# Three buffers, a later due time and copies in three pieces for the transposed convolution results of a two-layer hybrid block

## The chip, the cores and the metric

The kernel runs on one core of one Trainium2 chip. The time is the device time of one execution in microseconds (us). Three runs of the kernel before the change took 2925.31, 2929.0 and 2931.43 us; the median is 2929.0 us. One further execution was recorded by the hardware profiler, and all rows below come from it.

## The reference

Two layers (`DEPTH = 2`) work on 1024 latent tokens and 256 context tokens, each a vector of 1024. A layer normalizes and modulates its input, multiplies it by one wide matrix, splits the product in ten parts and feeds three branches: a state space scan (SSD) with a short convolution in front, attention with 12 query and 4 key heads, and a conformer branch with a long convolution. The branches are joined and multiplied by an output matrix. Cut to the part that the change touches:

```python
h = modulate(x, norm_g[i], shift[:, None], scale[:, None])
h_c = modulate(ctx, norm_g[i], shift_c, scale_c)
z, xbc, dtr, q, k, v, ga, ua, ub, gc = split_cols(h @ w_in[i])
...
# SSD branch: 1280 channels, a convolution of 5 taps along the tokens
xbc = jax.nn.silu(dwconv(xbc, conv_w, conv_b))
xs = xbc[..., :SSD_WIDTH].reshape(b, L, SSD_HEADS, SSD_HEAD_DIM)
Bm = xbc[..., SSD_WIDTH:SSD_WIDTH + SSD_BC]
Cm = xbc[..., SSD_WIDTH + SSD_BC:]
...
# conformer branch: 512 channels, a convolution of 31 taps
u = ua * jax.nn.sigmoid(ub)
u = jax.nn.silu(layernorm(dwconv(u, conv_w, conv_b), ln_g, ln_b))
u = u @ pw_w + pw_b
return u * jax.nn.silu(gate)
```

## The kernel before

All 1280 tokens (`T`) are held as ten tiles (`NT`) of 128. The normalized input lies in SBUF with its 1024 features on the partitions, in a high part `hh` and a low part `hl`, since every float32 product is built from three products of rounded parts (`mm3`, L193): for each of 8 slices of 128 features, high by high, high by low and low by high. Each result tile of 512 columns is thus 24 matmuls into one of the four PSUM buffers of the tag `m`.

Weights come through `wblock`. It loads a block in two halves: SP issues the DMA into a raw buffer `wr` (of which the pool has one), ScalarE copies it to the rounded high part (`wth`), and VectorE or GpSimd subtracts that to get the low part (`wtl`); `wth` and `wtl` have two buffers each. The second half's DMA waits until the raw buffer has been read.

A layer (`phase_b`) runs through these stages. First the k projection of ten token tiles, with weights (`wk`) from a pool of their own that was filled while the norms ran. Then that pool is closed (`ws.close()`) and two pools are opened on the same side of SBUF: `gp`, with the small buffers of gates and copies, and behind it `wt`, with the weights of all further projections. The v projection, a part with q and dt, and two parts of q follow; in between stand matmuls of the adaptive modulation (`ada_w`).

Then comes the convolution stage, nine blocks, alternately a pair of `xbc` tiles (128 channels each) and a pair `ub`, `ua`. The product of `xbc` is copied by ScalarE to a padded row `xpad`; `conv_x` (L557) makes five passes over it on VectorE into `xcv`, a tanh on ScalarE into `th`, and a last step on VectorE that multiplies the two. The products `ub` go through ScalarE's tanh into a tile of the same name and buffer `th` (one buffer), VectorE multiplies it by `ua` into `up`, and `conv_cm` makes 31 passes over `up` on VectorE into `cac`. Results 0 to 7 of `conv_x` are also transposed: TensorE turns ten squares of 128 by 128, four into a PSUM tile `x` (one buffer), four into `t` (two buffers) and two into `x` again; ScalarE copies them to SBUF, and DMAs take them to DRAM (`xt_d`, `bt_d`), from where the scan reads them by token. Gates (`g_t`, `g_o`), the tail of the conformer branch, the scan, attention and the output product come behind.

The order on each engine is not the order of the code. Every operation carries a due time in us, set by `at(...)`, and a list scheduler with a timeline of its own orders each engine's instructions by these. `XLAG` is the distance of a result's transposes from the due time of its convolution. Pools hand out buffers, and the waits between engines follow from which memory an operation reads and writes, also where a tile lies on memory that a closed pool had before.

Of the kernel before, what the change touches and what calls it, by code (L numbers as in the profile page):

```python
# [10 lines left out]
AF = mybir.ActivationFunctionType  # L11
# [18 lines left out]
A2B = 1  # L30
GATP = True
GB = 2
XLAG = 34
PVB = (4, 6)
DM = 1024
NLAT = 1024
# [2 lines left out]
NT = T // 128  # L39
# [121 lines left out]
def build(tc, a, out, depth=DEPTH, dump=None):  # L161
    nc = tc.nc
    es = ExitStack()
    V, S, G, P, Y = nc.vector, nc.scalar, nc.gpsimd, nc.tensor, nc.sync

    def at(us):
        tc.cur_priority = int(us * 100)

    def pool(st, name, bufs=1, **k):
        return st.enter_context(tc.tile_pool(name=name, bufs=bufs, **k))  # L170
# [3 lines left out]
    def mk(p, shape, tag, dt=F32, bufs=None):  # L174
        uid[0] += 1
        k = {} if bufs is None else {"bufs": bufs}
        return p.tile(shape, dt, tag=tag, name=f"{tag}_{uid[0]}", **k)
# [8 lines left out]
    def dr(shape, name, dt=F32):  # L186
        t = dp.tile(shape, dt, tag=name, name=name)
        if dump is not None:
            dump[name] = t
        return t  # L190
# [4 lines left out]
    def tr(o, i, idt):  # L195
        P.transpose(o, i, idt)  # L196

    def act(o, i, f, **k):
        S.activation(o, i, f, **k)  # L199

    def ts(e, o, i, s1, op0, s2=None, op1=None):
        if op1 is None:
            e.tensor_scalar(o, i, s1, None, op0)
        else:
            e.tensor_scalar(o, i, s1, s2, op0, op1)  # L205

    def stt(o, i, s, i1, op0, op1):
        V.scalar_tensor_tensor(o, i, s, i1, op0, op1)  # L208
# [24 lines left out]
    for l in range(depth):  # L233
        t = mk(cp, [128, NCOL], f"colc{l}")
        Y.dma_start(out=t, in_=a["colc"][l])
        colc.append(t)
        t = mk(cp, [128, NROW], f"rowc{l}")
# [18 lines left out]
    xt_d = dr([NT, 128, 768], "xt_d")  # L256
    bt_d = dr([NT, 128, 256], "bt_d")
# [176 lines left out]
    def phase_b(l, nh, b0, pp):  # L434
# [71 lines left out]
        gp = pool(st_r, f"gp{l}", side="right")  # L506
# [32 lines left out]
        xp_p = pool(s2, f"xp{l}")  # L539
# [17 lines left out]
        def conv_x(j, t0):  # L557
            xp = xps[j]
            at(t0)
            o = mk(xp_p, [128, 1282], "xcv", bufs=2)  # L560
            w = sw[:, 5 * j:5 * j + 5]
            ts(V, o, xp[:, 0:1282], w[:, 0:1], ALU.mult, sw[:, 50 + j:51 + j], ALU.add)
            for k in range(1, 5):
                at(t0 + 2 * k)
                stt(o, xp[:, k:k + 1282], w[:, k:k + 1], o, ALU.mult, ALU.add)
            at(t0 + 10)
            th = mk(up_p, [128, 1282], "th")
            act(th, o, AF.Tanh)
            stt(o, th, 1.0, o, ALU.add, ALU.mult)
            if j >= 6:  # L570
                d = bT_d[j - 6] if j < 8 else cT_d[j - 8]
                Y.dma_start(out=d[:, 0:1024], in_=o[:, 0:1024])
                Y.dma_start(out=d[:, 1024:1280], in_=o[:, 1026:1282])
            if j < 8:
                at(t0 + XLAG)
                sg = mk(gp, [128, NT, 128], "xsg")
                for ta in (0, 4, 8):
                    n = min(4, NT - ta)
                    ps = mk(*((pt, [128, 4, 128], "t") if ta == 4 else (px, [128, 4, 128], "x")))
                    for t in range(ta, ta + n):  # L580
                        c0 = t * 128 + (2 if t >= 8 else 0)
                        tr(ps[:, t - ta, :], o[:, c0:c0 + 128], idf)
                    act(sg[:, ta:ta + n, :], ps[:, 0:n, :], AF.Copy)
                if j < 6:
                    d = xt_d[:, :, 128 * j:128 * j + 128]
                else:
                    d = bt_d[:, :, 128 * (j - 6):128 * (j - 6) + 128]
                Y.dma_start(out=d.rearrange("t p f -> p t f"), in_=sg)

        def gate(ps, t0, n, d):  # L590
            th = mk(gp, [128, 512], "g_t", bufs=2)
# [31 lines left out]
        def block(i):  # L623
            u = FM_UNITS[i]
            u0 = b2 + 26 * i
            at(u0 - 20)
            w = wblock(wt, wt, a["wfm"][l, i], "wt", 2)
            tt = u0
            for m, (n, j) in enumerate(u):
                full = n == "xbc" or not last  # L630
                for t0, tn in ((0, 512), (512, 512), (1024, 256)):
                    if t0 >= 1024 and not full:
                        continue
                    at(tt)
                    ps = mk(pm, [128, 512], "m")
                    mm3(ps[:, 0:tn], lambda x, k: w[x][:, k, 128 * m:128 * m + 128],
                        lambda x, k: h[x][:, k, t0:t0 + tn], KT)
                    fm_fin(ps, n, j, t0, tn)
                    tt += 5.2 * tn / 512
                if n == "ua":  # L640
                    conv_cm(j, tt, CM_PACE)
                if n == "xbc":
                    conv_x(j, tt)
# [563 lines left out]
```

## Time and profile before

| what | value |
|---|---|
| median of three runs | 2929.0 us |
| profiled execution | 2925.86 us, span of its instructions 2924.0 us |
| TensorE busy | 2775.7 us, 95% of the span |
| VectorE busy | 2167.2 us, 74% |
| ScalarE busy | 1068.0 us, 37% |
| GpSimd busy | 1167.3 us, 40% |
| mean granted clock of TensorE | 0.976 of full speed |

Shares of busy time are means over the whole program. The convolution stage of layer 0 lies at about 250 to 600 us of the span, that of layer 1 at about 1770 to 2080 us; the v projections lie at about 98 us and 1655 us. The names in the rows are those of the program's tiles: `t<-msk,xcv` is a transpose of a convolution result into the PSUM tile `t` (a transpose is a matmul with an identity matrix, which lies in the tile `msk`), `m<-hh,wth` is a matmul of a projection into a tile `m`, `xsg<-x` is the copy of a transposed piece to SBUF. A time in square brackets is how long the engine stood idle before the instruction, with the operation that ended the wait.

### The profile page before, as it was taken

The page shows a single profiled execution, that of the slowest core. Times are in us where ns is not written, and L with a number is a line of the kernel's source. Part 1 is how long each engine was busy: PE and PEld are TensorE (multiplying, and loading weights), DVE is VectorE, ACT ScalarE, POOL GpSimd, SP SyncE. Part 2 cuts the span into 40 slices and gives each one's busy share as a digit, 9 for nine tenths or more (in the row PEclk, how much of TensorE's full clock was granted, in tenths as well). Part 3 has the DMA queues.
Part 4 walks back from the last instruction along what each step waited for, and adds up shares of the span by engine and source line. Part 5 has one row for each costly group of instructions (what it writes and reads, how often), then busy time and mean ns, then how long its engine had stood idle before and what let it go on. Part 6 is the DMA issues. An engine that isn't in the chain of part 4 may idle for free. (4 is left out here: it accounts for less than half of the span.)

```text
span 2924.0 us, 41060 instructions
## 1 busy us (share of the span) xinstructions
PE 2775.7 (95%) x15708; PEld 2058.5 (70%) x15708; DVE 2167.2 (74%) x2987; ACT 1068.0 (37%) x1801; POOL 1167.3 (40%) x832
## 2 busy tenths in 40 slices
PE   5999998999999999899999999999998999999998
PEld 3888876888855555565787998877886565555676
DVE  4576899973288889887545577999834889898744
ACT  4212221222245555454335322222223455644532
POOL 2244122232166767662112353122322676775111
PEclk8999998999999999999999999999999999999999
DMA  6541111223342323223745322113335232321654
GB/s 237 191 160 66 56 55 62 92 92 112 101 144 84 102 68 104 67 76 99 213 153 161 122 77 68 56 55 98 111 118 168 74 98 77 95 64 43 185 154 144
DMA packets 284035, 314.44 MB, mean 108 GB/s; under 512 B 27606, under 2 KB 219190, under 8 KB 282814
## 3 DMA queue, kind: packets, MB, share of 16 engines
q1 hardware_dynamic: 283838, 311.82, 33.5%
q8 instruction: 123, 2.02, 0.3%
q14 instruction: 74, 0.61, 0.1%
HBM read 236.25 MB, written 75.50 MB: 107 GB/s over the span
## 5 line engine op out<-in xcount | busy, mean ns | idle before, releaser
L193 PE MATMUL m<-hh,wth 128*128 128x512 f32 (+1 forms) x1440 | 534.9, 371 | 0.1
L193 PE MATMUL m<-hl,wth 128*128 128x512 f32 (+1 forms) x1440 | 533.4, 370 | 0.0
L193 PE MATMUL m<-hh,wtl 128*128 128x512 f32 (+1 forms) x1440 | 532.7, 370 | 0.0
L199 ACT ACTIVATE a_p<-m 128x512 f32<-128x512 f32 x492 | 289.0, 595 | 374.0 <-PE m L193 370.6
L208 DVE SCALAR_TENSOR_TENSOR cac<-up,cmw,cac 128x1295 f32<-128x1295 f32 (+1 forms) x240 | 385.4, 1627 | 2.0
L935 DVE TENSOR_REDUCE a_sm<-m 128x1 f32<-128x512 f32 (+1 forms) x600 | 332.5, 582 | 46.9 <-PE m L193 45.0
L359 POOL TENSOR_TENSOR wtl<-wr,wth 128x1024 fp32r<-128x1024 f32 x68 | 200.3, 2945 | 406.6 <-ACT wth L199 406.6
L193 PE MATMUL t<-a_p,vs 128*64 128x256 f32 x1968 | 324.0, 405 | 0.7 <-DVE a_rc L1010 0.3
L193 PEld LDWEIGHTS m<-hh,wth 128*128 128x128 f32 x1440 | 274.0, 190 | 48.0 <-ACT th L199 0.5
L193 PEld LDWEIGHTS m<-hh,wtl 128*128 128x128 f32 x1440 | 273.5, 190 | 48.3
L193 PEld LDWEIGHTS m<-hl,wth 128*128 128x128 f32 x1440 | 273.8, 190 | 47.4
L193 PE MATMUL m<-q_a,k_a 128*128 128x512 f32 (+1 forms) x656 | 259.7, 406 | 6.1 <-DVE a_sm L935 4.6
L193 PE MATMUL m<-k_a,q_a 128*128 128x512 f32 (+1 forms) x600 | 247.0, 437 | 13.6 <-DVE a_sm L935 9.8
L193 PE MATMUL m<-woh,yh 128*128 128x512 f32 x576 | 225.8, 395 | 8.2 <-issue 3.3
L193 PE MATMUL m<-woh,yl 128*128 128x512 f32 x576 | 228.8, 398 | 4.4 <-DVE yl L1099 4.3
L193 PE MATMUL m<-wol,yh 128*128 128x512 f32 x576 | 226.5, 394 | 0.0
L193 PE MATMUL m<-q_b,k_b 65*128 65x512 f32 (+1 forms) x656 | 218.8, 344 | 0.0
L193 PEld LDWEIGHTS m<-q_a,k_a 128*128 128x128 f32 x656 | 125.9, 192 | 107.1 <-issue 52.0
L193 PEld LDWEIGHTS t<-a_p,vs 128*64 128x64 f32 x1968 | 104.3, 136 | 133.9 <-issue 95.3
L193 PEld LDWEIGHTS m<-k_a,q_a 128*128 128x128 f32 x600 | 113.5, 195 | 113.3 <-issue 45.2
L199 ACT ACTIVATE wth<-wr 128x1024 fp32r<-128x1024 f32 (+1 forms) x84 | 89.3, 1064 | 256.3 <-DMA wr<-in_wfm 134.5
L193 PE MATMUL m<-wth,hh 128*128 128x256 f32 (+1 forms) x608 | 173.7, 288 | 0.6 <-DVE c_qn L474 0.5
(239 smaller groups left out, 5604.4 us busy)
## 6 DMA issues: line engine op xcount, KB each, us to landing
wr<-in_wfm SPq DMA_DIRECT2D x68, 512.0 KB, 3.6
s_cb<-cum_d SPq DMA_DIRECT2D x72, 384.0 KB, 3.7
ada_w<-in_adaw SPq DMA_DIRECT2D x32, 512.0 KB, 4.2
wor<-in_wout SPq DMA_DIRECT2D x64, 256.0 KB, 3.1
s_x<-xt_d SPq DMA_DIRECT2D x38, 384.0 KB, 3.0
yf<-ys_d SPq DMA_DIRECT2D x36, 384.0 KB, 4.0
yf<-ya_d SPq DMA_DIRECT2D x36, 384.0 KB, 4.2
yf<-yc_d SPq DMA_DIRECT2D x36, 256.0 KB, 2.9
```

Source lines behind the costliest of these rows:

```text
L193: P.matmul(o, l, r, start=start, stop=stop)
L199: S.activation(o, i, f, **k)
L208: V.scalar_tensor_tensor(o, i, s, i1, op0, op1)
L359: (e or G).tensor_tensor(lo[:, s], raw, hi[:, s].bitcast(F32), ALU.subtract)
L935: V.tensor_reduce(sm[:, 2 * x + t, j:j + 1], ps[:, 0:kn], axis=AX.X, op=ALU.max)
```

## The change

The due time of the transposes goes from 34 to 62 us behind the convolution's. `xcv` gets a third buffer. The tile `xsg` for a whole transposed result (ten squares, 5120 bytes per partition) goes; each of the three PSUM tiles is copied into a buffer of the tag `g_o`, of which there are two and which the gates use too (2048 bytes per partition each), and every piece has a DMA of its own.

```diff
-XLAG = 34
+XLAG = 62
...
-            o = mk(xp_p, [128, 1282], "xcv", bufs=2)
+            o = mk(xp_p, [128, 1282], "xcv", bufs=3)
...
             if j < 8:
                 at(t0 + XLAG)
-                sg = mk(gp, [128, NT, 128], "xsg")
+                if j < 6:
+                    d = xt_d[:, :, 128 * j:128 * j + 128]
+                else:
+                    d = bt_d[:, :, 128 * (j - 6):128 * (j - 6) + 128]
                 for ta in (0, 4, 8):
                     n = min(4, NT - ta)
                     ps = mk(*((pt, [128, 4, 128], "t") if ta == 4 else (px, [128, 4, 128], "x")))
                     for t in range(ta, ta + n):
                         c0 = t * 128 + (2 if t >= 8 else 0)
                         tr(ps[:, t - ta, :], o[:, c0:c0 + 128], idf)
-                    act(sg[:, ta:ta + n, :], ps[:, 0:n, :], AF.Copy)
-                if j < 6:
-                    d = xt_d[:, :, 128 * j:128 * j + 128]
-                else:
-                    d = bt_d[:, :, 128 * (j - 6):128 * (j - 6) + 128]
-                Y.dma_start(out=d.rearrange("t p f -> p t f"), in_=sg)
+                    sg = mk(gp, [128, 512], "g_o", bufs=2)[:, 0:128 * n].rearrange("p (t f) -> p t f", t=n)
+                    act(sg, ps[:, 0:n, :], AF.Copy)
+                    Y.dma_start(out=d[ta:ta + n].rearrange("t p f -> p t f"), in_=sg)
```

How the engines' orders change is seen at three places. The first is SP, the engine that issues the DMAs, at the end of layer 0's k projection: `wr_151` and `wr_152` are the two halves of the v weights, `k_d` the stores of finished k tiles, and behind each row stands what it waits for. Before:

```order
L278 DMA ada_w_389_2554<-in_adaw 128x1024 [waits DMAHW7_49,DMAHW3_49,PE_49]
L357 DMA wr_151_945<-in_wtm 128x1024 [waits DVE_49,DMAHW0_49,Activation_49,Pool_49]
L484 DMA k_d_127<-c_t1_129_809 128x256 [waits DMAHW1_49,DVE_49]
L484 DMA k_d_127<-c_t1_135_849 128x256 [waits DVE_49]
L278 DMA ada_w_390_2558<-in_adaw 128x1024 [waits DMAHW6_49,PE_49]
L278 DMA ada_w_391_2562<-in_adaw 128x1024 [waits DMAHW7_49,DMAHW4_49,PE_49]
L357 DMA wr_152_949<-in_wtm 128x1024 [waits DMAHW5_49,DMAHW0_49,DVE_49]
L484 DMA k_d_127<-c_t1_141_889 128x256 [waits DVE_49]
```

And now:

```order
L484 DMA k_d_127<-c_t1_129_809 128x256 [waits DMAHW0_49,DVE_49]
L484 DMA k_d_127<-c_t1_135_849 128x256 [waits DMAHW1_49,DVE_49]
L278 DMA ada_w_390_2558<-in_adaw 128x1024 [waits DMAHW6_49,PE_49]
L278 DMA ada_w_391_2562<-in_adaw 128x1024 [waits DMAHW7_49,PE_49]
L357 DMA wr_151_945<-in_wtm 128x1024 [waits PE_49,DMAHW4_49,Activation_49,Pool_49]
L484 DMA k_d_127<-c_t1_141_889 128x256 [waits DMAHW5_49,DVE_49]
L278 DMA ada_w_395_2574<-in_adaw 128x4x256 [waits DMAHW2_49,PE_49]
L278 DMA ada_w_396_2580<-in_adaw 128x4x256 [waits DMAHW3_49,PE_49]
L484 DMA k_d_127<-c_t1_147_929 128x256 [waits DMAHW0_49,DVE_49]
L308 DMA gt_d0_148<-ada_g_392_2566 2x1024 [waits DMAHW1_49,DVE_49]
L304 DMA ada_b_426_2727<-in_adab 2x1024
L357 DMA wr_152_949<-in_wtm 128x1024 [waits DMAHW4_49,DVE_49]
```

The first half's load stood ahead of two k stores and two `ada_w` loads and waited for VectorE, ScalarE and GpSimd; it now stands behind them and waits for TensorE, ScalarE and GpSimd. Its TensorE wait is for the last matmul of the k projection. Four more rows stand between the two halves.

The second place is TensorE in layer 0, where in the trace of before the wait at 352.77 us lies. `xcv_477` (now `xcv_481`) is the convolution result of channel tile 2, `xcv_487` (now `xcv_493`) that of channel tile 3, and `m` is a product of the next projection. Before:

```order
L193 MATMUL m_501_3499<-hh_19_153,wtl_494_3411 128x512
L196 MATMUL x_480_3284<-msk_2_74,xcv_477_3274 128x128 x4
L196 MATMUL t_481_3290<-msk_2_74,xcv_477_3274 128x128 x4
L196 MATMUL t_491_3399<-msk_2_74,xcv_487_3383 128x128 x4
L196 MATMUL x_482_3296<-msk_2_74,xcv_477_3274 128x128 x2
L193 MATMUL m_503_3529<-hh_19_153,wth_493_3410 128x512
```

And now:

```order
L193 MATMUL m_509_3515<-hh_19_153,wtl_502_3427 128x512
L196 MATMUL x_483_3291<-msk_2_74,xcv_481_3282 128x128 x4
L196 MATMUL t_485_3299<-msk_2_74,xcv_481_3282 128x128 x4
L196 MATMUL t_497_3412<-msk_2_74,xcv_493_3395 128x128 x4
L193 MATMUL m_511_3545<-hh_19_153,wth_501_3426 128x512
```

The last two squares of tile 2 (`x` x2) have left this place; they come some 170 rows later. The first pieces of tile 2 and the `t` piece of tile 3 stand where they stood.

The third place is TensorE where the wait at 493.94 us lies, with the results of channel tiles 6 and 7 (`xcv_549` and `xcv_559`, now `xcv_561` and `xcv_573`) and two long convolution results (`cac`). Before:

```order
L193 MATMUL m_573_4363<-hh_19_153,wtl_566_4275 128x512
L196 MATMUL x_552_4146<-msk_2_74,xcv_549_4134 128x128 x4
L196 MATMUL t_553_4152<-msk_2_74,xcv_549_4134 128x128 x4
L196 MATMUL x_554_4158<-msk_2_74,xcv_549_4134 128x128 x2
L196 MATMUL x_562_4257<-msk_2_74,xcv_559_4245 128x128 x4
L196 MATMUL t_563_4263<-msk_2_74,xcv_559_4245 128x128 x4
L196 MATMUL t_710_5641<-msk_2_74,cac0_429_2748 128x128
L196 MATMUL t_710_5641<-msk_2_74,cac1_430_2749 128x128
L193 MATMUL m_575_4393<-hh_19_153,wth_565_4274 128x512
```

And now:

```order
L193 MATMUL m_589_4395<-hh_19_153,wtl_582_4307 128x512
L196 MATMUL x_563_4169<-msk_2_74,xcv_561_4158 128x128 x4
L196 MATMUL t_565_4177<-msk_2_74,xcv_561_4158 128x128 x4
L196 MATMUL x_567_4185<-msk_2_74,xcv_561_4158 128x128 x2
L196 MATMUL x_575_4284<-msk_2_74,xcv_573_4273 128x128 x4
L196 MATMUL t_577_4292<-msk_2_74,xcv_573_4273 128x128 x4
L196 MATMUL t_726_5673<-msk_2_74,cac0_429_2748 128x128
L196 MATMUL t_726_5673<-msk_2_74,cac1_430_2749 128x128
L193 MATMUL m_591_4425<-hh_19_153,wth_581_4306 128x512
```

Here the rows are the same, but for the numbers of the buffers. Elsewhere in layer 0 the pieces of tiles 0 and 1, the rest of tile 3 and those of tile 5, except for `t`, and the last piece of tile 7 stand some 140 to 240 rows later than before.

## Rows read from the trace of the kernel before

**Rows 1.** TensorE's waits, 250 to 800 us: waiter <- waited for: us, times, longest

```profile
PE x L196 <- DVE xcv L208: 13.3, 2, 11.1
PE x L196 <- ACT xsg L199: 5.7, 3, 4.9
PE t L196 <- DVE xcv L208: 4.2, 1, 4.2
PE t L196 <- DVE cac L208: 2.3, 1, 2.3
```

**Rows 2.** TensorE's waits, 1700 to 2200 us

```profile
PE t L196 <- DVE xcv L208: 11.7, 3, 6.1
```

**Rows 3.** VectorE's waits, 296 to 610 us

```profile
DVE up L208 <- PE m L193: 9.1, 5, 3.3
```

**Rows 4.** VectorE's waits, 1813 to 2075 us

```profile
DVE up L208 <- PE m L193: 4.9, 1, 4.9
```

**Rows 5.** Stretches: length, busy us (instructions) by engine, granted clock, DMA share, GB/s

```profile
100.00:250.00 150.00, 149.64 (x1172) 129.50 (x1171) 92.28 (x240) 30.69 (x62) 62.37 (x69) 1.00 0.49 159
420.00:500.00 80.00, 66.41 (x325) 55.73 (x324) 76.50 (x51) 15.05 (x24) 17.82 (x13) 0.87 0.21 67
1655.00:1800.00 145.00, 144.51 (x1059) 138.02 (x1058) 98.58 (x216) 32.21 (x60) 63.01 (x66) 1.00 0.26 84
```

**Rows 6.** Timeline of layer 0: start, length, instruction [idle before <- releaser]

```profile
352.75 1.36 ACT L199 ACTIVATE th<-m 128x512 f32<-128x512 f32 x3 [1.08 <-DVE xcv L208]
352.77 1.12 PE L196 MATMUL t<-msk,xcv 128*128 128x128 f32 x4 [4.15 <-DVE xcv L208]
353.96 0.78 PE L193 MATMUL m<-hh,wth 128*128 128x512 f32 x1
```

**Rows 7.** Timeline near 493 us

```profile
493.91 1.36 ACT L199 ACTIVATE th<-m 128x512 f32<-128x512 f32 x3 [1.56 <-DVE xcv L208]
493.94 1.11 PE L196 MATMUL x<-msk,xcv 128*128 128x128 f32 x4 [11.05 <-DVE xcv L208]
```

**Rows 8.** Timeline before the first long convolution

```profile
294.89 0.60 PE L196 MATMUL x<-msk,xcv 128*128 128x128 f32 x4
299.12 0.42 DVE L208 SCALAR_TENSOR_TENSOR up<-th,m 128x256 f32<-128x256 f32 x1 [3.27 <-PE m L193]
```

**Rows 9.** Timeline of the v weights, layer 0

```profile
91.73 0.33 SPq L357 DMA_DIRECT2D wr<-in_wtm  x1
99.38 0.33 SPq L357 DMA_DIRECT2D wr<-in_wtm  x1
96.96 1.06 ACT L199 ACTIVATE wth<-wr 128x1024 fp32r<-128x1024 f32 x1 [3.70 <-DMA wr<-in_wtm]
104.43 1.06 ACT L199 ACTIVATE wth<-wr 128x1024 fp32r<-128x1024 f32 x1 [5.89 <-DMA wr<-in_wtm]
98.05 1.31 DVE L359 TENSOR_TENSOR wtl<-wr,wth 128x1024 fp32r<-128x1024 f32 x1 [0.58 <-ACT wth L199]
105.52 1.23 DVE L359 TENSOR_TENSOR wtl<-wr,wth 128x1024 fp32r<-128x1024 f32 x1 [1.52 <-ACT wth L199]
97.67 0.39 PE L193 MATMUL m<-wkh,hl 128*128 128x256 f32 x1
98.07 0.62 PE L193 MATMUL m<-wth,hh 128*128 128x256 f32 x3
103.52 1.91 PE L280 MATMUL t<-ada_w,sc 128*32 128x512 f32 x8
```

**Rows 10.** Timeline of the v weights, layer 1

```profile
1648.50 0.33 SPq L357 DMA_DIRECT2D wr<-in_wtm  x1
1652.30 1.06 ACT L199 ACTIVATE wth<-wr 128x1024 fp32r<-128x1024 f32 x1 [2.62 <-DMA k_d<-c_t]
1654.86 0.27 PE L193 MATMUL m<-wkh,hl 128*128 128x256 f32 x1
```

**Rows 11.** Landing times of the copies from xsg to DRAM

```profile
DMA to landing us min/median/max: 3.6/3.9/5.8
```

## The prediction

> **What bounds the kernel now.** I read the page first: TensorE is busy for 2775.7 of 2924.0 us (95%) and the chain that ended last runs mostly along its projections and convolutions, so what counts is where TensorE waits. Next came its waits over the convolution stage of each layer. In layer 0 it stands 13.3 + 5.7 + 4.2 = 23.2 us in front of transposes of convolution results (tile `xcv`), held by VectorE's `xcv` or by ScalarE's `xsg` copy, and 2.3 us in front of a transpose of `cac` [rows 1]; in layer 1 it stands 11.7 us for `xcv` [rows 2]. Together 34.9 us of the kind that the change addresses. Third, the same table for VectorE: from 296 to 610 us its waits for TensorE add to only 9.1 us in five places [rows 3], and from 1813 to 2075 to 4.9 us in one [rows 4]. In the convolution stage VectorE is therefore the engine that is nearly full, and TensorE's waits are the slack that it leaves: in 420 to 500 us VectorE works 76.50 of 80 us, TensorE 66.41 at a granted clock of 0.87 [rows 5]. Ahead of that stage it is the other way round: TensorE has 149.64 busy of 150 us in 100 to 250, and 144.51 of 145 in 1655 to 1800 [rows 5]. A microsecond lost there is lost for good; a microsecond won in the convolution stage is won only as far as VectorE can use it.
>
> **The change part by part.** Three edits: the transposes of a result get a due time 62 instead of 34 us behind its convolution; `xcv` has three buffers for two; the tile `xsg` of 5120 bytes per partition goes, and each third of a result is copied into a 2048-byte buffer of the tag `g_o` and sent off on its own.
>
> *The stalls at the transposes.* The order of the changed program decides which of them move. At the first big stall (352.77 us, 4.15 us idle) the `t` transpose of the youngest result still stands at the same row of TensorE; only the third piece of the older one is gone. At the longest (493.94 us, 11.05 us idle) nothing has moved at all; at the second, between these two, one of two transposes of the youngest result has moved. Even a full move would give little: at these three places the four PSUM buffers of tag `m` are all full, three with `ub` products and one with the first `ua` product, and they become free through ScalarE's `th<-m`. That one waits for the tile `th`, which VectorE's last `xcv` step releases, the very step that the transposes wait for. The rows show it: `th<-m` starts at 352.75, the transposes at 352.77 [rows 6]; 493.91 and 493.94 [rows 7]. Behind the first stall the next product starts at 353.96 [rows 6]; without any transposes it would wait for the first of three evictions, 352.75 + 1.36/3, or 353.2. So a stall gives back 0.3 to 0.8 us to TensorE, and later products that VectorE waits for come earlier by as much. To this I add the transposes of the first result (0.60 us for four [rows 8], ten in all, so 1.1 counting overlap), which leave the place in front of the `ua` product for which VectorE idles 3.27 us at 299.12 [rows 8]. Carried along VectorE's order this makes about 1.1 us at the start, 1.4 behind the first stall, 2.6 behind the second and 4 at the end of layer 0's stage. Bounds: nothing, and the 9.1 us that VectorE idles there in all [rows 3]. I take 4. In layer 1 VectorE idles once, 4.9 us at the head of the stage [rows 4], in front of anything the moved transposes could speed up; bounds 0 and 4.9, I take 0.5.
>
> *The buffers.* `xcv` was not what anybody waited to get free: VectorE's table has no row for it [rows 3, 4]. Its third buffer costs and gives nothing.
>
> *What the missing 5120 bytes do.* The pool of the projection weights (`wt`) is opened right behind the pool of `xsg` and `g_o`. With `xsg` gone, it slides by 5120 bytes, and its raw buffer `wr` comes to lie partly over the k weights (`wk`), which TensorE reads until its last k product. In the order before, the load of the first half of the v weights waits for the engines of the norms, not TensorE; in the changed order its waits begin with TensorE, and it stands four rows lower. The same holds in layer 1; no other weight load's conditions change so. In layer 0 the load was issued at 91.73 us, ScalarE rounded it at 96.96 (5.23 later), VectorE had the low part under way at 98.05, the second half was issued at 99.38 and its low part was begun at 105.52 [rows 9]. The last k product starts at 97.67 and takes 0.39 [rows 9], so the new issue is at 98.06 at the earliest, 6.3 us later. The second half uses the same raw buffer, so it moves along: 98.1 + 5.2 = 103.3 for the rounding, its 1.06 and the 1.23 of the low part make 105.7 for the second issue and, by the 104.43 - 99.38 = 5.05 us of before, 110.8 and then 111.9 for the second low part, 6.4 us behind 105.52. TensorE ran four v tiles side by side and was at their first half until the second came; its rest of these tiles hangs on that low part. The eight `ada_w` products of 1.91 us [rows 9] fill part of the hole but were due anyway. Between the two loads SP now has a k store, two loads of `ada_w` and another store, so 6.4 is the low end and two more microseconds the high one, 8.5. I take 7. The engine is full from there to the convolutions [rows 5]: all of it is passed on.
>
> In layer 1 the load was issued at 1648.50 and rounded at 1652.30, 3.80 later [rows 10]. The last k product starts at 1654.86 and takes 0.27 [rows 10]: issue at 1655.1, 6.6 later. VectorE and ScalarE follow as before. TensorE had mixed a few v products into the last k tile, so that this ends a little earlier when they are gone; bounds 5 and 7, I take 6. Could this be free? Only if TensorE had other work there, and the q and dt tiles have their weights behind the v weights in the same two buffers.
>
> *The pieces.* There were 16 copies to DRAM, there are 48, 32 more issues on SP. TensorE's transposes and ScalarE's copies stay as many. With two `g_o` buffers the third copy of a result needs the first piece landed, and the landings of the whole tile took 3.6 to 5.8 us [rows 11]. In ScalarE's order the `th<-xcv` step, for which VectorE is due, follows such a third copy at three places in layer 0; there the transposes stand in TensorE's order well ahead of the products that the step is due with. So I count nothing, with bounds of 0 and 16 × 0.4 = 6 us, a tenth of a landing at each result.
>
> The Trainium skill, "DMA: Bandwidth & Descriptors", section "Rules for kernel authors", advises to coalesce many small transfers into one large one, and its section on the anatomy of a DMA gives each a fixed cost of about 2.0 us. By that, as an estimate, 32 more transfers carry 64 us of fixed cost if an engine waits for each of them. The trace shows the landings but, in front of TensorE, only 5.7 us of waits for `xsg` in layer 0 [rows 1], so I give the rule only the third rival below.
>
> *Sum.* + 7 + 6 - 4 - 0.5 = + 8.5 us. The profiled execution took 2925.86 us (2.0 of it around the span), 3.1 below the median of the runs, 2929.0; from its own time the sum gives 2934.4, from the median 2937.5. I forecast 2937.
>
> **The rivals.** First, faster: the 34.9 us of waits are real idle time of the fullest engine, and the rule "TensorE bounds" would have them go. With the two loads' 13 us against them this gives 2929 + 13 - 34.9 = 2907. Against it: VectorE's 9.1 and 4.9 us and the equal starts in [rows 6, 7]. 7%. Second, no measurable change: the late v loads are covered after all, or TensorE's delay is given back in front of the convolutions, where VectorE idles; with half of the 13 us gone and the 4.5 won it ends at 2931, within a band of 2925 to 2934. For it: the other weights have long leads. Against it: TensorE's 149.64 of 150 us [rows 5]. 25%. Third, slower by more: a third copy waits at the head of ScalarE for its buffer and holds `th<-xcv`, hence VectorE, hence every later tap. It decides once a landing ends later than the `th<-xcv` was due; at two thirds of the 16 results by 1 us each it adds 11 us: 2948. For it: VectorE has no slack to absorb it; against it: `th<-m` starts with `xcv` as its releaser [rows 6, 7], so ScalarE stands idle and waiting for VectorE there, not the other way. 10%. Fourth, the change does nothing of what it says at the stalls (VectorE's order eats the 4.5 as well): 2929 + 13 = 2942, 10%, and a part of my own side.
>
> **How the numbers follow.** My forecast has 48%, its own range is 2931 to 2945 (the loads between 6.4 + 5 and 8.5 + 7, the gain between 0 and 9). About 0.2%, 5.9 us, is what a measurement of this kernel tells from no change, so "same" is 2923.1 to 2934.9. Faster takes most of the first rival and a little of the second: 9%. Same takes most of the second and the low fifth of my own: 30%. Slower has the rest of mine, the third and fourth: 61%. The range of 8 in 10 leaves out the first rival and a part of the third: 2925 to 2947.
>
> **What would show it.** Right: the first v load is issued within 1 us of the last k product, in both layers; TensorE then has a wait of 4 to 6 us for `wth` or `wtl` in front of the v products; the v tiles end 6 to 8 us later; VectorE's 9.1 us shrink to about 5; the waits for `xcv` in [rows 1, 2] partly turn into waits for `th<-m` evictions with nearly the same ends. Wrong: v loads that leave before the last k product, or no TensorE wait there; a convolution stage that becomes shorter by more than 9.1 us; waits of ScalarE on landings of `g_o` in front of `th<-xcv`.

## The result, and the profile after

The changed kernel took 2942.35 us (median of four runs, 2940.33 to 2945.62) where the kernel before took 2927.15 (2924.24 to 2931.43): a ratio of 1.0058, 95% interval 1.0042 to 1.0074, some 15 us slower. The forecast was 2937 us, 8 over the median known then.

The changed kernel's own profile (span 2938.6 us, clock 0.974) differs most from the first one where the v weights come in. The next rows are of the changed kernel in layer 0, from SP, ScalarE, VectorE and TensorE, with the columns of [rows 9]:

```profile
98.07 0.33 SPq L357 DMA_DIRECT2D wr<-in_wtm  x1
108.62 0.36 SPq L357 DMA_DIRECT2D wr<-in_wtm  x1
...
105.03 1.19 ACT L199 ACTIVATE ada_g<-t 2x512 f32<-2x512 f32 x2 [6.77 <-PE t L280]
106.12 1.04 ACT L199 ACTIVATE wth<-wr 128x1024 fp32r<-128x1024 f32 x1
112.67 1.06 ACT L199 ACTIVATE wth<-wr 128x1024 fp32r<-128x1024 f32 x1 [5.50 <-DMA wr<-in_wtm]
...
107.39 1.21 DVE L359 TENSOR_TENSOR wtl<-wr,wth 128x1024 fp32r<-128x1024 f32 x1
113.75 1.23 DVE L359 TENSOR_TENSOR wtl<-wr,wth 128x1024 fp32r<-128x1024 f32 x1 [5.16 <-ACT wth L199]
...
97.46 0.39 PE L193 MATMUL m<-wkh,hl 128*128 128x256 f32 x1
99.75 1.92 PE L280 MATMUL t<-ada_w,sc 128*32 128x512 f32 x4 [1.91 <-DMA ada_w<-in_adaw]
107.22 1.22 PE L193 MATMUL m<-wth,hh 128*128 128x256 f32 x4 [2.23 <-ACT wth L199]
```

The last k product starts at 97.46, and SP issues the first v load at 98.07, where it had left at 91.73 [rows 9]. ScalarE rounds it only at 106.12: two `ada_g` activations stand in front, and they wait for `ada_w` products that wait for their own load. The second half's low part is begun at 113.75 instead of 105.52 [rows 9], and TensorE's first v products start at 107.22 instead of 98.07. The next rows are stretches of the same trace, in the columns of [rows 5], around the v weights of both layers:

```profile
98.00:107.00 9.00, 3.84 (x8) 0.37 (x8) 3.85 (x9) 2.22 (x4) 1.99 (x3) 0.60 0.75 241
107.00:113.00 6.00, 5.79 (x29) 4.75 (x30) 1.60 (x2) 0.50 (x2) 0.00 (x0) 0.50 0.68 215
1662.00:1668.00 6.00, 0.60 (x5) 0.40 (x4) 4.15 (x13) 1.44 (x2) 3.77 (x4) 0.87 0.46 153
1668.00:1675.00 7.00, 6.97 (x38) 6.67 (x39) 2.55 (x3) 1.06 (x1) 0.00 (x0) 0.62 0.30 96
```

From 98 to 107 TensorE is busy for 3.84 of 9 us, and in the 6 us behind that it works at a granted clock of 0.50, which is 1.2 instead of 2.4 GHz. In layer 1 it is busy for 0.60 of 6 us and then gets 0.62. Layer 1 in single rows of the changed kernel, to set beside [rows 10]:

```profile
1663.05 0.34 SPq L357 DMA_DIRECT2D wr<-in_wtm  x1
1669.02 0.33 SPq L357 DMA_DIRECT2D wr<-in_wtm  x1
...
1662.12 0.28 PE L193 MATMUL m<-wkh,hl 128*128 128x256 f32 x1
1667.79 1.22 PE L193 MATMUL m<-wth,hh 128*128 128x256 f32 x4 [5.39 <-ACT wth L199]
```

The load leaves at 1663.05, 0.65 us behind the end of the last k product, and TensorE stands 5.39 us until the first half is rounded; in the kernel before, its only wait around these products was 0.5 us.

The waits of TensorE in the changed kernel, over the windows of [rows 1] and [rows 2] (the second group from 1800 to 2100):

```profile
PE x L196 <- DVE xcv L208: 10.4, 2, 9.8
PE x L196 <- ACT g_o L199: 5.6, 4, 4.0
PE t L196 <- DVE xcv L208: 3.4, 2, 3.0
PE t L196 <- DVE cac L208: 3.1, 2, 2.2
```

```profile
PE x L196 <- ACT g_o L199: 4.5, 2, 2.9
PE t L196 <- DVE xcv L208: 3.0, 2, 2.1
PE m L193 <- ACT th L199: 2.2, 2, 1.9
```

In layer 0 the waits for `xcv` and for the copies fall from 23.2 to 19.4 us, in layer 1 from 11.7 us to 9.7 including two waits for `th`. The long ones stay. Here are the first big stall in the changed kernel, beside [rows 6], and VectorE's waits for `m` over the whole convolution stage of layer 0, first in the kernel before, then in the changed one:

```profile
360.75 1.36 ACT L199 ACTIVATE th<-m 128x512 f32<-128x512 f32 x3 [1.61 <-DVE xcv L208]
...
360.78 0.66 PE L196 MATMUL t<-msk,xcv 128*128 128x128 f32 x4 [2.99 <-DVE xcv L208]
```

```profile
DVE up L208 <- PE m L193: 18.3, 7, 4.9
```

```profile
DVE up L208 <- PE m L193: 14.2, 5, 4.9
```

The eviction of the `ub` tiles and the transpose still start together. VectorE's waits shrink by 4.1 us. Over 305 to 620 us, the stretch of [rows 3] moved by 9 us, they are 5.0 us, where about 5 were forecast.

### The profile page after: what moved, and what is told of

Same layout as the page of the kernel before. It is cut to its first block, busy times and chain, and to the rows that moved or that the text cites. A ratio compares the mean times of both kernels' runs of the same rounds, so it can differ in the third digit from the quotient of the medians.

```text
span 2938.6 us, 41147 instructions
## 1 busy us (share of the span) xinstructions
PE 2781.1 (95%) x15708; PEld 2063.5 (70%) x15708; DVE 2168.5 (74%) x2987; ACT 1067.0 (36%) x1801; POOL 1175.9 (40%) x832
## 5 line engine op out<-in xcount | busy, mean ns | idle before, releaser
L359 POOL TENSOR_TENSOR wtl<-wr,wth 128x1024 fp32r<-128x1024 f32 x68 | 208.0, 3059 | 422.2 <-ACT wth L199 422.1
L199 ACT ACTIVATE wth<-wr 128x1024 fp32r<-128x1024 f32 (+1 forms) x84 | 89.3, 1063 | 286.9 <-DMA wr<-in_wfm 157.0
```

The costliest lines, as they stand in the source:

```text
L359: (e or G).tensor_tensor(lo[:, s], raw, hi[:, s].bitcast(F32), ALU.subtract)
```

## Where the time goes, stage by stage

The table gives the length of five stages, each from the start of a first instruction to the end of a last one (or its start, where it is a first one), in one trace per kernel. The second traces of both kernels are of two runs told of below.

| kernel | k and v, layer 0 | `xpad` to last `cac` tap, layer 0 | first `yh` to first k product | k and v, layer 1 | `xpad` to last `cac` tap, layer 1 |
|---|---|---|---|---|---|
| before | 88.6 | 357.5 | 252.0 | 67.9 | 310.0 |
| before, second trace | 89.9 | 355.7 | 254.3 | 68.5 | 307.8 |
| changed | 98.9 | 353.9 | 254.5 | 75.5 | 308.6 |
| changed, second trace | 98.3 | 353.2 | 256.5 | 78.8 | 308.7 |
| slide | 99.1 | 357.6 | 254.5 | 78.0 | 307.8 |
| rawfirst | 98.3 | 353.4 | 260.3 | 76.3 | 307.5 |
| fix | 88.7 | 353.0 | 255.4 | 71.0 | 307.6 |
| fix_before | 89.3 | 356.4 | 254.6 | 71.2 | 306.8 |
| pieces_pad | 89.7 | 355.3 | 258.0 | 70.9 | 308.1 |

k and v run from the first k product to the last copy `c_v` of a v tile. Two traces of one kernel differ by up to 3.3 us in a stage, so a single difference under 4 us says little; four traces against four say more. The four with late loads (both of the changed kernel, `slide`, `rawfirst`) have a mean of 98.6 and 77.1 us for k and v in the two layers, the four with early loads (both of before, `fix`, `fix_before`) 89.1 and 69.7. In layer 0's convolution stage the four traces that have all three edits take 353.0 to 353.9 us, the four that have none 355.7 to 357.6, which is 3.4 us by their means; in layer 1 both means are 308.1.

## The experiments

**The slide alone, and the bytes of the raw buffer.** `slide` takes `xsg` out of the kernel before's pool `gp`, so that the weight pool moves and nothing else is edited; `rawfirst` is the changed kernel with the raw buffer laid out first in the weight pool, away from the k weights.

```diff
 slide (against before)
-                sg = mk(gp, [128, NT, 128], "xsg")
+                sg = mk(xp_p, [128, NT, 128], "xsg")
...
 rawfirst (against the changed kernel, in wblock; the line with n moves up)
+        raws = [mk(rp, [128, n, shape[2]], rtag, bufs=rbufs)]
         hi = mk(p, shape, tag + "h", F32R, bufs=bufs)
         lo = mk(p, shape, tag + "l", F32R, bufs=bufs)
...
-            raw = mk(rp, [128, n, shape[2]], rtag, bufs=rbufs)
+            raw = raws[0] if k == 0 else mk(rp, [128, n, shape[2]], rtag, bufs=rbufs)
```

> The kernel before with one edit: the tile xsg is taken from the pool of the convolution rows (xp) instead of gp, so that the weight pool slides by 5120 bytes over the k weights as in the changed kernel; transposes, due times and copies stay. Theory (the v weights load late): both v projections are delayed as in the changed kernel, 9.6 and 7.6 us, and nothing is won at the convolutions: 17 us over before, 2944 us (2940 to 2948). Rival (the pieces and their blocked copies cost the time, the loads matter little): 2927 to 2931.

> The changed kernel with one edit: in the weight pool the raw buffer is laid out first, so that its bytes no longer lie over the k weights; the second low buffer lies there instead. Theory A (the bytes of the raw buffer decide, as the prediction put it): the first v load leaves early again and the time falls by 14 to 17 us, to 2925 to 2928. Theory B (the pool's whole range decides: the first load into a pool waits for every pool that lay under any part of it): the first v load is issued behind the last k product as before, and the time stays at 2942 (2939 to 2945).

Measured for `slide`: 2941.65 us against 2932.64 of the kernel before on the same chip, ratio 1.0032 (1.0021 to 1.0044), slower by 9 us. The time lies in the expected range only because the kernel before ran slower beside it (2932.64) than the 2927 us that the 17 were added to. Its waits of TensorE around the v weights of layer 0, and below the dots of layer 1, are close to those of the changed kernel (there 3.3, 2.2 and 5.4):

```profile
PE t L280 <- DMA ada_w<-in_adaw: 4.3, 2, 2.6
PE m L193 <- ACT wth L199: 2.2, 1, 2.2
...
PE m L193 <- ACT wth L199: 5.5, 1, 5.5
```

For `rawfirst`: 2937.47 us, ratio 1.0012 (1.0000 to 1.0023), between the two ranges expected. The trace decides. Its last k product starts at 96.28 in layer 0; these are its two v loads there and TensorE's wait in layer 1:

```profile
96.89 0.33 SPq L358 DMA_DIRECT2D wr<-in_wtm  x1
107.47 0.36 SPq L358 DMA_DIRECT2D wr<-in_wtm  x1
...
PE m L193 <- ACT wth L199: 5.5, 1, 5.5
```

The load still leaves behind the last k product although its bytes lie elsewhere, and in the program it waits for the same TensorE instruction as in the changed kernel. So in this framework it is the range of the whole pool that counts: while any part of it lies over the k weights, its first load waits for them. That falsifies the prediction's reason (the raw buffer's own place), not its effect. Both traces have the long k and v stages. The order of every engine in `rawfirst` is that of the changed kernel, and still it came out 0.4% nearer to the kernel before than that did in two other sessions; this difference stays unexplained, and the changed kernel itself was not run beside it.

**The loads set free.** `fix` is the changed kernel, `fix_before` the kernel before, both with the weight pool split on the same memory, so that the raw buffer is a pool that touches neither norms nor k weights.

```diff
-        wt = pool(st_r, f"wt{l}", side="right")
+        w1 = pool(st_r, f"w1{l}", side="right")
+        w0 = pool(st_r, f"w0{l}", side="right")
+        wt = pool(st_r, f"wt{l}", side="right")
+        nb = [0]
+        def wp(src, *e):
+            nb[0] += 1
+            return wblock((w1, w0)[nb[0] % 2], wt, src, "wt", 1, *e)
...
-        w = wblock(wt, wt, a["wtm"][l, 1], "wt", 2, V)
+        w = wp(a["wtm"][l, 1], V)
... (and the two later calls of wblock with wt in the same way)
```

> The changed kernel with the weight pool split in three on the same memory: the second buffers of the weights next to gp (over the k weights), the first buffers below, the raw buffer in a pool of its own below these, where neither the norms nor the k weights lay. Theory (late v loads cost 17 us, the convolution stages win 3.6 + 1.4): the time falls by 17 to 20 us, to 2922 to 2926, with v tiles that end no later than in the kernel before. Rival (pieces cost the time): 2938 to 2943.

> The kernel before with the weight pool split in three in the same way, so that it stands beside the split version of the changed kernel with equal v loads. Theory: within 2 us of before, 2925 to 2928 (the v projections wait only 0.7 and 0.5 us there); the split changed kernel is 3 to 6 us faster than this one, all of it in the convolution stages. Rival (the pieces cost time): this one is faster than the split changed kernel by 10 us or more.

Measured in one session with the two above: `fix` 2922.10 us, ratio 0.9958 (0.9947 to 0.9970); `fix_before` 2925.71, ratio 0.9969 (0.9957 to 0.9981). The rows of `fix` show the first load leaving at 6.32 and both halves rounded in time; the last row is TensorE's only wait from 85 to 140 us:

```profile
6.32 0.67 SPq L357 DMA_DIRECT2D wr<-in_wtm  x1
...
92.62 1.06 ACT L199 ACTIVATE wth<-wr 128x1024 fp32r<-128x1024 f32 x1 [3.83 <-DVE c_ss L205]
100.10 1.06 ACT L199 ACTIVATE wth<-wr 128x1024 fp32r<-128x1024 f32 x1 [5.86 <-DMA wr<-in_wtm]
...
PE t L280 <- DMA ada_w<-in_adaw: 0.8, 1, 0.8
```

The four kernels make a square. With the order of before, late loads cost 2941.65 - 2925.71 = 15.9 us; with the changed order 2937.47 - 2922.10 = 15.4 us. Against the kernel before itself, though, `slide` lost only 9.0 us: `fix_before`, expected within 2 us of it, was 6.9 us faster, and its trace doesn't show where. So the price of the late loads is 9 to 16 us by whole times, and 17 by the means of the table. By the square the three edits win 3.6 us with free loads and 4.2 us with late ones, but neither is clear of noise: five runs of `fix` (2921.5 to 2925.8) and of `fix_before` (2921.0 to 2930.1) overlap, and the 4.2 rest on `rawfirst` in the place of the changed kernel, which took no less than `slide` in its own sessions. The gain is shown by the 3.4 us of the table.

**The third buffer, the due time, the pieces.** `fix_b2` is `fix` with two `xcv` buffers (`bufs=3` to `bufs=2`), `lag2` the kernel before with the due time alone (`XLAG = 62`), `pieces_pad` the kernel before with the pieces alone and a tile in `gp` that keeps the weight pool where it was:

```diff
 pieces_pad (against before, beside the copies in pieces as in the change)
         gp = pool(st_r, f"gp{l}", side="right")
+        at(b0 - 6)
+        G.memset(mk(gp, [128, 1280], "pad")[:, 0:1], 0.0)
```

> The split version of the changed kernel (weight pool in three parts) with two xcv buffers instead of three; due time 62 and pieces stay. Theory (nobody waits for an xcv buffer): as with three, 2922 us (2920 to 2925), VectorE without a wait for an xcv buffer. Rival (with the late transposes a result is held so long that the convolution of the next but one waits for its buffer): VectorE shows waits for TensorE's transposes in front of the first xcv pass, and the time rises by 4 to 10 us, to 2926 to 2932.

> The kernel before with the due time of the transposes at 62 instead of 34 alone (two xcv buffers, one xsg and one copy). Theory (the later due time moves the transposes of results 0, 1 and 5 and is the source of the gain at the convolutions): layer 0's convolution stage 2 to 4 us shorter than in the kernel before, the v projections as before, time 1 to 5 us under before. Rival (the gain came from the third buffer): the stage is as long as before or longer, time 0 to 6 us over before.

> The kernel before with the copies in three pieces alone (due time 34, two xcv buffers), and a tile of 5120 bytes left in gp so that the weight pool keeps its place. Theory (the pieces cost nothing): within 3 us of before, v tiles where they ended before. Rival (third copies wait for landings and hold ScalarE): 4 to 11 us over before, with ScalarE waits for the landing of g_o in front of th<-xcv.

Measured: `fix_b2` 2970.86 us (1.0134, 1.0115 to 1.0153), 49 over `fix`; `lag2` 2966.72, 35 over before (1.0124, 1.0105 to 1.0142); `pieces_pad` 2928.87 against 2932.06 (0.9997, 0.9985 to 1.0008). The pieces are free, with TensorE's waits as before. The other two went as neither theory had it: the time rose by far more than the 10 and 6 us of the rivals, and not because a convolution waits for a buffer. In `fix_b2` VectorE has no such row, as its waits from 250 to 615 us show:

```profile
DVE up L208 <- PE m L193: 16.3, 6, 4.7
DVE xcv L208 <- ACT th L199: 2.9, 2, 1.5
DVE xcv L205 <- ACT xpad L199: 2.6, 1, 2.6
```

TensorE stands instead, in layer 0 three times for 11 to 12 us and in layer 1 three times for 32.2 us together; two of them:

```profile
370.03 1.12 PE L196 MATMUL x<-msk,xcv 128*128 128x128 f32 x4 [12.05 <-DVE xcv L208]
...
513.59 1.11 PE L196 MATMUL x<-msk,xcv 128*128 128x128 f32 x4 [11.32 <-DVE xcv L208]
```

In its order two pieces each of results 3 and 5 stand at the stalls, in front of the next product, where the changed kernel has one; a result must be out of its buffer before the next but one is begun, so with two buffers its transposes can't all be put later. `lag2` has such waits too, from 250 to 800 us, to be read against [rows 1]:

```profile
PE x L196 <- DVE xcv L208: 34.8, 4, 11.7
```

**The shared tanh tile.** `fix_th2` is `fix_b2` with a tile of its own for the tanh of `ub`, `th2_34` the same with the due time back at 34, `th3` the same as `fix_th2` with three buffers, where `xn` had to share the gates' `g_t` for room.

```diff
 fix_th2
-                    tub[j] = mk(up_p, [128, 1282], "th")
+                    tub[j] = mk(up_p, [128, 1282], "tu")
...
 th3, further
-                    xn = mk(gp, [128, 512], "xn", bufs=1)
+                    xn = mk(gp, [128, 512], "g_t", bufs=2)
```

> The same with two xcv buffers, and the tanh of the ub products in a tile of its own (tu) instead of sharing th with the convolutions' tanh. Theory (at the three big stalls the m tiles are full because their eviction waits for th, and VectorE bounds the stage): ScalarE evicts the ub products earlier, TensorE's waits of 4.2, 4.9 and 11 us shrink or move to the ua products, and since VectorE has at most 9.1 us of waits in layer 0 the time falls by 1 to 5 us against the version with two buffers, to 2917 to 2922. Rival (the transposes themselves hold TensorE): waits and time stay within 1 us.

> The version with split weight pool, two xcv buffers and a tanh tile of its own for ub, with the due time of the transposes back at 34. Theory (two things hold TensorE at the stalls, the full m tiles and the transposes of a result that VectorE has not finished; either alone suffices): the m tiles are evicted early, but the transposes wait for VectorE again, TensorE shows 8 to 20 us of waits for xcv in layer 0, and the time is 3 to 15 us over the version with due time 62, 2918 to 2930. Rival (only the shared tanh tile mattered): same time as with 62, 2913 to 2918, with no long wait for xcv.

> The version with split weight pool, tanh tile of its own and due time 62, with three xcv buffers (xn shares the gates' buffers to make room). Theory (with the m tiles evicted early no convolution waits for an xcv buffer at two either): the same as with two, 2912 to 2918. Rival (the third buffer is worth as much here as with the shared tanh tile, 49 us there): 2900 or less.

Measured: `fix_th2` 2915.22 us (0.9950, 0.9934 to 0.9967), 56 under `fix_b2`; `th2_34` 2911.88 (0.9943, 0.9928 to 0.9958), the fastest of all, 18 us under the kernel before of its session. The nearest kernel that shares the tile, with the same due time, two `xcv` buffers and free loads, is `fix_before` (0.9969 in another session): by the ratios the tile of its own is worth some 8 us, an estimate, as the copies in pieces differ too. The due time 62 shows no gain once the tile is not shared (0.9950 against 0.9943), and the theory that the transposes alone suffice to hold TensorE fell. The waits of TensorE for transposes in `th2_34`, from 250 to 800 us, to be read against [rows 1]:

```profile
PE x L196 <- ACT g_o L199: 6.4, 2, 3.9
PE t L196 <- DVE cac L208: 2.6, 2, 2.1
PE x L196 <- DVE xcv L208: 2.0, 1, 2.0
```

The long waits for `xcv` are gone although the transposes are due as in the kernel before. ScalarE's rows of `th2_34` show why: a `ub` product leaves PSUM at 344.52, 11 us ahead of the convolution's tanh, and at 402.52 right behind one, without the wait for VectorE's last `xcv` step that `th<-m` had in [rows 6, 7].

```profile
344.52 0.60 ACT L199 ACTIVATE tu<-m 128x512 f32<-128x512 f32 x1
...
355.87 1.28 ACT L199 ACTIVATE th<-xcv 128x1282 f32<-128x1282 f32 x1 [8.09 <-DVE xcv L208]
...
402.52 0.58 ACT L199 ACTIVATE tu<-m 128x512 f32<-128x512 f32 x1
```

What that is worth shows in the stretches, first of the kernel before, then of `th2_34`:

```profile
250.00:612.00 362.00, 336.50 (x1722) 284.94 (x1721) 330.37 (x227) 74.68 (x113) 83.45 (x64) 0.96 0.20 67
612.00:800.00 188.00, 187.75 (x1005) 159.78 (x1003) 70.97 (x143) 43.99 (x71) 41.56 (x28) 1.00 0.30 103
```

```profile
250.00:612.00 362.00, 349.70 (x1826) 301.02 (x1825) 336.10 (x237) 77.39 (x119) 103.19 (x68) 0.98 0.22 69
612.00:800.00 188.00, 182.64 (x976) 155.06 (x975) 82.85 (x158) 48.72 (x82) 45.95 (x33) 0.98 0.38 122
```

TensorE does 1826 matmuls in the convolution stage instead of 1722, though VectorE ends its last `cac` tap no earlier, at 604.83 in the kernel before and 606.03 in `th2_34`. The 104 matmuls are work of the next stage, which was full (187.75 of 188 us), and the last gate of layer 0 ends 16.6 us earlier (12.8 against the second trace of the kernel before).

`th3` took 2970.05 us and tells nothing of the third buffer: TensorE is busy for only 165.67 of the 188 us from 612 on, where the conformer's tail with the shared `xn` runs, so the loan of that buffer is mixed into it.

**Second traces.** The changed kernel and the kernel before were run once more as they are.

> The changed kernel as it is, run beside the kernel before once more, since the kernel before ran between 2923 and 2939 us in the last sessions: 0.4 to 0.7% slower than before. Its trace again with v tiles that end 9 to 10 and 7 to 8 us later after the last k product, and a stage from yh of layer 0 to the first k product of layer 1 that is within 3 us of the kernel before either way, if the 2.5 us of the first trace were chance.

> The kernel before as it is, for a second trace of it. If its first trace was a quick draw in the output stage of layer 0 (252.0 us from the first yh to the first k product of layer 1, against 254.0 to 260.3 in the ten other kernels, whose code is the same there), this trace shows 254 us or more there, and a time of 2928 to 2935 us. If the later v loads slow that stage by an effect of their own, it is 252 us again. The v projections and the convolution stages as in the first trace, within 1 us.

The changed kernel: 2943.88 us against 2929.86, ratio 1.0049 (1.0033 to 1.0065). The single run of the kernel before took 2923.16, below the range expected, and its stages differ from the first trace by up to 2.3 us, not 1. Its output stage took 254.3 us, not 252.0 again (table), so the 2.5 us that the changed kernel seemed to lose there are no more than two traces of one kernel differ by.

## Why the prediction was right, and where not

*The loads.* Right in mechanism, issue time and sign, though the reason given, the raw buffer's own place, was falsified by `rawfirst`. The issue at 98.07, with 98.06 forecast at the earliest, agrees so closely by luck, since the last k product came 0.2 us earlier. By the traces the size was too small. In layer 0 the step "98.1 + 5.2 = 103.3 for the rounding" failed: it was 106.12, since ScalarE's order had put `ada_g` in front, so the second low part came 8.2 us late, at the top of the range, not 6.4. From the first traces the last v tile ends 9.6 us late, where 7 were taken.

But "its rest of these tiles hangs on that low part" is not what the trace shows: from 107.22 on TensorE waits for nothing until the last v product. It lost its time ahead of that, 1.91 + 1.39 us for `ada_w` loads and 2.23 for the first half, where it had stood 0.7 in the kernel before, and by its clock, which the sum left out. An estimate from the stretches above: 5.5 - 0.7 = 4.8 us of idle time and (1 - 0.60) x 3.84 + (1 - 0.50) x 5.79 = 4.4 us for the clock, 9.2 of the 9.6. That 7 was near is thus partly luck; whether TensorE would have waited for the second half at full clock is not shown. In layer 1 the term of 6 measured 7.6 (75.5 - 67.9): in the same way 5.4 - 0.5 = 4.9 us of idle time and (1 - 0.62) x 6.97 = 2.6 for the clock. That makes 17.2 for the two terms by the first traces, against the 13 forecast; the square of four kernels gives 15 to 16, and `slide` against the kernel before 9.

*The convolution stages.* The term of 4 in layer 0 measured 3.6 against the first trace of the kernel before and 1.8 against its second; four traces against four give 3.4. The 0.5 of layer 1 measured 1.4 (310.0 - 308.6), but `slide`, which has none of the edits, shows 2.2 there too, and four against four give nothing. With 2.5 us in the output stage the first traces thus add to 9.6 + 7.6 - 3.6 - 1.4 + 2.5 = 14.7, and their spans are 14.6 apart; the stretches between these stages, at most 1.1 us apart each, cancel.

*What did not follow.* "Its third buffer costs and gives nothing" was wrong: without it the due time costs 35 to 49 us. VectorE's missing waits didn't show that, because with two buffers the scheduler puts the transposes at an earlier place in TensorE's order, as in `fix_b2`, and then it is TensorE that waits. "Won only as far as VectorE can use it", with the 9.1 us of [rows 3] for a ceiling, was wrong too. Behind the convolution stage TensorE is full, and in `th2_34`, where the full `m` tiles hold it less, it does some of that work ahead. The first rival's idle time is thus partly there to be won, only not by this change, since the full `m` tiles hold TensorE, as the prediction said from [rows 6, 7]. The third rival (blocked copies) was half right. ScalarE did wait at the head of its order for pieces to land, which the prediction had named as a sign of being wrong; here are two such waits of the changed kernel, one in each layer, and the `th<-xcv` behind each:

```profile
354.27 0.39 ACT L199 ACTIVATE g_o<-x 128x256 f32<-128x256 f32 x1 [5.29 <-DMA xt_d<-g_o]
357.87 1.27 ACT L199 ACTIVATE th<-xcv 128x1282 f32<-128x1282 f32 x1 [3.21 <-DVE xcv L208]
...
1994.88 0.38 ACT L199 ACTIVATE g_o<-x 128x256 f32<-128x256 f32 x1 [9.53 <-DMA xt_d<-g_o]
1995.16 1.27 ACT L199 ACTIVATE th<-xcv 128x1282 f32<-128x1282 f32 x1
```

In layer 0 ScalarE then still waited for VectorE; in layer 1 the tanh was held, but VectorE's waits for `th` over that stage grew only from 2.9 to 3.2 us. With the ratio of `pieces_pad` that leaves the pieces no price. The Trainium skill ("DMA: Bandwidth & Descriptors", section "Rules for kernel authors") advises to coalesce many small transfers and speaks of mostly overhead under 64 KB. The pieces, at 256 and 128 KB each, lie above that, and that they cost nothing that can be measured here (ratio 0.9997) agrees with it. The 2.0 us that the prediction takes from the same page of the Trainium skill stand there in a section on transfers that GpSimd issues, while SP issues these; its sum does not use them.

## What to carry to other kernels

A tile that is taken out of one pool moves every pool behind it: look which loads then wait for the memory's last readers, since one late load a layer in front of a full TensorE cost more here (9 to 16 us) than the edits won (3.4). A stall that two waits end at the same moment must be traced to what they share (here one tanh buffer), and only undoing that showed what the stall was worth. Idle time of an engine that is full in the next stage can be won there, even where another engine bounds the present stage.

## What was not expected of the hardware

Behind 9 us with 3.84 busy, TensorE worked at half its clock for the next 6 us although it was busy for 5.79 of them, and a first load that left 6.3 us later moved the last v tile by 9.6. The kernel before took 2923 to 2939 us in three sessions, and stages scatter by up to 3.3 us between two traces of one kernel, so an effect of 4 us needs kernels that run side by side.
